# Twelve DRAM copies issued by ScalarE instead of GpSimd, with an order table of their own

## The chip, the cores and the metric

The kernel runs on one core of one Trainium2 chip. The metric is the device time of one execution in microseconds. The core has a matmul engine (TensorE, PE), VectorE (DVE), ScalarE (ACT), GpSimd (POOL) and SyncE (SP), each with an instruction queue of its own that is worked off in order, and 16 DMA engines that all queues' transfers share.

## The reference

One decoder layer on 512 tokens of width 1024 in float32: two token mixers in parallel, a gated merge, an output projection, layer norm, then a gated FFN of width 2816 with a short convolution, and layer norm again. Cut to what matters:

```python
def conv_ffn(x, w_up, conv_w, w_down):
    h = causal_dwconv(x @ w_up, conv_w)          # w_up 1024 x 5632, conv of width 3
    gate, val = jnp.split(h, 2, axis=-1)
    return (jax.nn.silu(gate) * val) @ w_down    # w_down 2816 x 1024

def reference(x, w_in, ...):
    h = x @ w_in                                 # 1024 -> 5408
    y_a = nsa_attention(...) @ w_nsa_out         # sparse attention, 8 heads
    y_b = gated_deltanet(...) @ w_gdn_out        # gated DeltaNet, 4 heads
    mix = (sigmoid(gate_a) * y_a + sigmoid(gate_b) * y_b) @ w_o
    x = layer_norm(ALPHA * x + mix, ln1_g, ln1_b)
    return layer_norm(ALPHA * x + conv_ffn(x, ffn_w_up, ffn_conv_w, ffn_w_down), ln2_g, ln2_b)
```

## The kernel before

Every large product is made in three passes: a float32 operand is cast to a high part (`wh`, `mh`, ScalarE or GpSimd) and the rest is a low part (`wl`, `ml`, VectorE), and PE adds high·high, high·low and low·high. A weight tile is loaded by SyncE into `raw` (3 buffers), cast into `wh` (3 buffers) and its rest into `wl` (3 buffers); then come 12 matmuls of it.

Three products are made with 7 half-size products in place of 8: the output projection with w_o, the down projection, and 7 of the 22 pairs of column groups of the up projection (`SEVEN`: pairs 5, 7, ... 17; function `seven`, one tile of 128x512 for each half-size product). The other pairs are made by `plain` with whole products. A half-size product of this kind needs sums of blocks of the weights. They are made by DMA in DRAM: each of `osum` (512 rows of 2 KB), `usum` (896 rows) and `wsum` (1408 rows) gets four sums by eight transfers. Four of the eight are plain copies (from the weight, or from one sum to the next), four add a block of the weight to what the copy left. Sums 0 and 1 are copied and added to; sum 2 is a copy of sum 1 with a block added, sum 3 a copy of sum 2 with a block added. All 24 are issued by GpSimd in before. SyncE loads the finished sums like other weights (`raw<-osum`, `raw<-usum`, `raw<-wsum`).

In time: until about 400 us the input projection and the two mixers run side by side, with `osum` and `usum` made beside them; then the merge (`mt`, L1147) and the w_o product with loads of `osum`; from about 450 the layer norm, which writes `mh` and `ml`, and with it the first up products; up to 700 the FFN's up projection, in which groups of `plain` and `seven` alternate and `wsum` is made; then the down projection, which reads `wsum`, and the last norm.

In `seven` the seven half-size products of a pair go through PSUM tiles `px`, `pz0` and `pz1`; after each, ScalarE or VectorE moves or adds it into the collecting tiles `wf0` and `wf1` (one buffer each), and the next product into the same PSUM tile waits for that. `gated` makes the convolution: `fa` by ScalarE (L1545), then two steps of VectorE (L1548). `fth` is the gate times the value: ScalarE (L1606), VectorE (L1607), GpSimd (L1608); `pha` is its high part (L1612, L1619), `pla` its low part.

The order of all instructions on each engine is fixed by a table `QUEUES`: for each engine a list of numbers, in which the n-th instruction that the program writes for this engine is number n. `queues` adds an ordering without a semaphore between neighbours of each list. So an instruction that waits holds back all that the table puts behind it on its engine.

Of the kernel before, what the change touches and what calls it, by code (L numbers as in the profile page):

```python
# [143 lines left out]
391-392 377 393 378 394 379-382 395 383 299-300 396-399 444-445 301 446-450 400-401 416 402-406 417 407-411 418-433
456 434-439 457-459 451 316-317 320 318 321-323 319 460-463 324-327 464-466 328 332-339 329-331 467-472 513 340-347
473-475 348-355 452 476-477 501 356-359 384-387 478-479 514-519 412-415 502-503 520-521 504 522-525 440 453 441 454
442 455 443 526-531 723-725 532 480-484 505 507-508 726-729 533 730 506 485 731 534-536 486-487 509-510 541 732 542
488-489 733-734 490 751-752 735-736 491-492 543 753 737 754-755 493 544 511 494 512 738 495 546-547 739 496 545 497
740 756-757 548 498-499 549 758-760 500 550-551 761 560-561 762 741 763-764 742-744 562 565 552 745 566 746 563-564
537 591 765 592 766 538-540 567 767 581-582 768 553-554 593 568 594-597 569 555 570 598-600 556-557 583 558 585 584  # L150
559 586 571 796 769-772 572-574 587 575 601 773 602 797-798 588 576 799 774 589-590 603-607 800-803 577-578 651 579
804-805 580 652 806 608-611 807-810 620 811 653-654 621 612 622-625 812-813 626 613 814-817 864 614 865 615 627 641
628-630 616-618 642 619 866-868 643-644 869-870 645-646 631 871-875 632 876-877 633 647-650 699-700 818 634-635
878-879 636 880-882 701-702 704-705 637 703 883 638 884 639 885-886 706 640 887 718-719 707-709 720-722 819 838-839
710 655-657 659-660 658 661-662 840-843 854-855 663-666 711-716 667-678 856 717 844 858 845 679-686 860 846-849 859
687-694 861 857 1053 850 695-698 747-748 862 749-750 863 1054 936-938 851 939-946 775 1055-1057 776-779 947-949 780
1058-1059 950 781 951-953 782 954-957 977 783 978 958 784-785 1060 959 1072 786-787 979 1073 852 980 853 981 788
982-984 789-790 985-986 791-792 987-992 793 1061 993-994 1001 794-795 1062 995-1000 1002-1012 1074 820 824-825 821-822
1075 823 1076 1101 1063 1013 826-829 1102 830-831 1103 832-833 1104-1108 1064 1029-1031 1014 1032 1065 1033-1034 1066
1035-1039 1067 1015 834 1040-1042 835 1043 1016 1044-1045 836 1046 837 1047-1049 1017 1050-1052 1068 1018-1019 888-891  # L160
1069 1077-1082 1070 1083-1100 1020-1023 1071 1024 1109-1112 892 896-897 893 898 894 899 895 1203 1205-1208 900-903
1204 1113 1209 1114-1115 904-905 908-915 906-907 1116 1219 1117 1210 1220 1118 1211 1119-1120 1212-1215 1221 916-923
1222-1223 1216 1121 1224 924-931 1122 1217 932-935 1225 1123 1233-1234 1124-1125 960 1126-1128 961 1129-1130 962-963
1131-1133 1218 1134-1136 964 1226 965 1235-1236 1227-1228 966 1141-1143 1238 1144-1145 967-968 1239 1146-1149 969 1237
970 1240 1150-1152 971-972 1153-1154 1252 1179 1241 973 1242 1253 1155 1180 974 1181-1182 975 1243 1254-1256 976
1156-1157 1183-1184 1158 1257 1159 1185 1160-1161 1186 1258 1244 1162 1187 1163-1164 1188-1190 1245 1191-1193 1246
1025-1026 1137-1139 1259 1140 1260-1261 1027 1262 1028 1273 1247 1194 1274 1195 1283 1196-1197 1248-1249 1198-1199
1284 1250 1200 1285 1251 1201 1263 1202 1165 1275 1169 1286-1287 1277 1307 1288 1278 1264 1170 1308-1310 1289-1290
1311 1166 1279 1167 1171 1280 1172-1173 1168 1174 1276 1403-1404 1312-1317 1175 1405 1176-1178 1265 1281 1406 1282
1407 1318 1266-1267 1319 1408 1320 1268 1291 1269 1409 1292 1270-1272 1321-1327 1229 1328-1329 1293-1294 1231 1410  # L170
1422-1423 1330 1295 1230 1296 1411 1424-1425 1412 1426 1413 1427 1297-1299 1232 1300-1303 1414 1428 1304 1379 1305
1415 1380 1416-1417 1306 1418 1429-1432 1443-1444 1381-1386 1419-1421 1387-1389 1433-1434 1445 1447-1448 1435 1390
1436 1391 1437 1331 1449 1332 1446 1453 1438-1439 1450-1452 1440 1454 1392 1477 1393-1394 1441 1395-1397 1455 1458
1478 1459 1479 1442 1480 1398 1460 1456-1457 1461-1462 1333 1463 1399 1481 1400-1401 1482-1483 1472-1473 1484-1485
1402 1474-1476 1334 1486-1491 1501-1502 1464-1465 1492 1466-1467 1582 1468 1503 1469-1470 1583 1517 1493 1518
1494-1495 1471 1504 1335 1505-1506 1336-1342 1519 1507 1521-1522 1496-1497 1508 1343-1346 1520 1509-1511 1584
1347-1358 1523 1512-1514 1498 1585 1544 1499 1545 1500 1359-1366 1524-1525 1546-1548 1367-1374 1515 1610 1549-1550
1375-1378 1526 1611 1586-1587 1527 1551-1552 1612 1588 1563 1528 1553 1529 1613 1554 1530 1589 1564 1590-1591 1614
# [189 lines left out]
def body(ctx: ExitStack, tc: tile.TileContext, d, out):  # L368
# [140 lines left out]
    def sums_o():  # L509
# [4 lines left out]
        for (to, src, add), u in zip(todo, SUMS):  # L514
            i = G.dma_start(out=osum[to], in_=src, **({"accum_op": OP.add} if add else {}))
# [1251 lines left out]
```

## Time and profile before

| | before |
|---|---|
| median of 3 runs | 837.82 us (837.53 to 840.38) |
| profiled execution | 837.5 us, its span 835.7 us, 12479 instructions |
| mean clock granted to PE | 0.992 |
| busy: PE, DVE, ACT, POOL | 97%, 77%, 52%, 23% |
| DMA | 139.8 MB moved; hardware queue q1 34.8% of 16 engines, GpSimd's queue q0 24.2% |

The span runs from the first to the last instruction of the profiled execution. Busy times are sums over an engine. q1 holds what SyncE issues; q0 what GpSimd issues. A line such as L1504 is a line of the kernel before; in the kernel after the same code stands one line further on. `a <- b` in a row of waits reads: the first waited for the second.

### The profile page before, as it was taken

What the parts mean: (1) busy time and instruction counts of PE and PEld (TensorE: products, weight loads), DVE (VectorE), ACT (ScalarE), POOL (GpSimd) and SP (SyncE); (2) the same over time, 40 slices, a digit from 0 to 9 for tenths busy, and PEclk for the clock granted to TensorE, in tenths of its full rate; (3) what the DMA queues carried; (4) which work ended last, traced back from release to release, by engine and by line L of the source; (5) the groups of instructions that cost most, each with busy time, mean ns of one, the idle gap of its engine ahead of it and who ended that gap; (6) DMA issues with size and microseconds to landing.
All of it is one profiled execution on the core that took longest, in us unless ns stands there. A gap on an engine that the chain in (4) does not pass through costs nothing.

```text
span 835.7 us, 12479 instructions
## 1 busy us (share of the span) xinstructions
PE 806.7 (97%) x4390; PEld 681.9 (82%) x4390; DVE 641.3 (77%) x1391; ACT 432.1 (52%) x965; POOL 195.2 (23%) x186
## 2 busy tenths in 40 slices
PE   9999999999999999999899999989999999999996
PEld 8788888778788888888787898968788888888875
DVE  5668689889678965565479879857777887788788
ACT  4463686774576764332344235543645654565541
POOL 0334825042275211332100112220011121100001
PEclk9999999999999999999999999999999999999999
DMA  8326129078246936446566697789483468475674
GB/s 277 95 86 214 30 76 249 26 192 186 56 131 156 187 90 153 151 127 153 213 252 203 239 185 234 182 220 201 137 276 114 140 156 197 138 206 173 205 238 148
DMA packets 53406, 139.80 MB, mean 167 GB/s; under 512 B 3936, under 2 KB 5088, under 8 KB 53088
## 3 DMA queue, kind: packets, MB, share of 16 engines
q1 hardware_dynamic: 36064, 92.88, 34.8%
q0 software_dynamic: 17280, 46.14, 24.2%
q8 instruction: 34, 0.56, 0.3%
q14 instruction: 28, 0.23, 0.1%
HBM read 136.91 MB, written 48.23 MB: 222 GB/s over the span
## 4 chain that ended last, share of the span: by engine, by line
PE 77%; DVE 10%; DMA 7%; ACT 3%; issue 2%; POOL 0%; SPq 0%; DVEq 0%; ACTq 0%; POOLq 0%
PE pu L1568 15%; PE gps L495 8%; PE gps L497 8%; PE gps L498 8%; PE px L1645 4%; PE px L1515 4%; PE pz L1645 4%; PE pz L1515 3%; DMA raw<-in_up 2%; PE pout L1115 2%; PE aps L1101 2%; DMA raw<-usum 2%; PE pu L1645 2%; PE pm L495 2%; PE pm L497 2%
## 5 line engine op out<-in xcount | busy, mean ns | idle before, releaser
L495 PE MATMUL gps<-xh,wh 128*128 128x512 f32 x320 | 125.2, 402 | 3.1 <-ACT mt L1147 2.3
L498 PE MATMUL gps<-xh,wl 128*128 128x512 f32 x320 | 125.7, 400 | 0.0
L497 PE MATMUL gps<-xl,wh 128*128 128x512 f32 x320 | 125.1, 399 | 0.0
L1568 PE MATMUL pu<-mh,wh 128*128 128x512 f32 x208 | 80.4, 398 | 2.2 <-ACT wh L1562 2.2
L1568 PE MATMUL pu<-mh,wl 128*128 128x512 f32 x208 | 79.7, 399 | 1.0 <-DVE wl L1563 1.0
L1568 PE MATMUL pu<-ml,wh 128*128 128x512 f32 x208 | 79.8, 396 | 0.0
L1608 POOL TENSOR_TENSOR fth<-fth,fa 128x512 f32<-128x512 f32 x22 | 32.4, 1474 | 197.3 <-DVE fth L1607 150.6
L495 PEld LDWEIGHTS gps<-xh,wh 128*128 128x128 f32 x320 | 60.5, 190 | 15.1 <-issue 3.3
L485 DVE TENSOR_TENSOR wl<-raw,wh 128x512 fp32r<-128x512 f32 x66 | 48.4, 738 | 29.7 <-PE gps L498 13.6
L498 PEld LDWEIGHTS gps<-xh,wl 128*128 128x128 f32 x320 | 60.5, 190 | 11.5 <-POOL wl L485 0.6
L497 PEld LDWEIGHTS gps<-xl,wh 128*128 128x128 f32 x320 | 60.5, 190 | 10.4
L1470 ACT ACTIVATE wh<-raw 128x512 fp32r<-128x512 f32 x67 | 39.9, 626 | 38.9 <-PE px L1645 9.5
L1562 ACT ACTIVATE wh<-raw 128x512 fp32r<-128x512 f32 x52 | 32.6, 628 | 51.5 <-PE pu L1568 41.5
L1471 DVE TENSOR_TENSOR wl<-raw,wh 128x512 fp32r<-128x512 f32 x67 | 44.4, 691 | 16.7 <-ACT wh L1470 16.6
L1563 DVE TENSOR_TENSOR wl<-raw,wh 128x512 fp32r<-128x512 f32 x52 | 38.2, 739 | 21.3 <-ACT wh L1562 18.1
L1504 ACT ACTIVATE wh<-raw 128x512 fp32r<-128x512 f32 x49 | 30.6, 628 | 40.2 <-PE px L1515 15.2
L1548 DVE SCALAR_TENSOR_TENSOR fa<-pu,fcw,fa 128x511 f32<-128x511 f32 (+1 forms) x60 | 44.3, 745 | 7.7 <-ACT fa L1545 7.4
L481 ACT ACTIVATE wh<-raw 128x512 fp32r<-128x512 f32 x46 | 28.8, 627 | 38.4 <-PE gps L497 29.6
L1568 PEld LDWEIGHTS pu<-mh,wh 128*128 128x128 f32 x208 | 39.7, 191 | 8.8 <-ACT wh L1562 2.6
L1568 PEld LDWEIGHTS pu<-mh,wl 128*128 128x128 f32 x208 | 39.6, 191 | 8.8 <-DVE wl L1563 2.6
L485 POOL TENSOR_TENSOR wl<-raw,wh 128x512 fp32r<-128x512 f32 x30 | 41.8, 1413 | 19.9 <-PE gps L498 5.4
L1568 PEld LDWEIGHTS pu<-ml,wh 128*128 128x128 f32 x208 | 39.6, 190 | 6.2
(498 smaller groups left out, 2252.8 us busy)
## 6 DMA issues: line engine op xcount, KB each, us to landing
raw<-in_wT SPq DMA_DIRECT2D x40, 512.0 KB, 3.7
raw<-in_up SPq DMA_DIRECT2D x37, 512.0 KB, 4.6
wsum<-in_down POOLq DMA_DIRECT2D x6, 2816.0 KB, 21.7
usum<-in_up POOLq DMA_DIRECT2D x6, 1792.0 KB, 15.8
raw<-wsum SPq DMA_DIRECT2D x20, 512.0 KB, 3.6
raw<-in_down SPq DMA_DIRECT2D x15, 512.0 KB, 4.3
osum<-in_wo POOLq DMA_DIRECT2D x6, 1024.0 KB, 10.8
wsum<-wsum POOLq DMA_DIRECT2D x2, 2816.0 KB, 15.0
```

What stands on the lines that cost most here:

```text
L485: eng.tensor_tensor(wl, r, wh.bitcast(F32), op=OP.subtract)
L495: i = PE.matmul(ps, wh[k], mh_(k), start=(k == 0), stop=False)
L497: PE.matmul(ps, wh[k], ml_(k), start=False, stop=False)
L498: PE.matmul(ps, wl[k], mh_(k), start=False, stop=(k == n - 1))
L1470: A.activation(hi, raw[:, i], AF.Copy)
L1471: V.tensor_tensor(lo, raw[:, i], hi.bitcast(F32), op=OP.subtract)
L1515: stop=k == 3 and w is lo) if False else PE.matmul(
L1548: V.scalar_tensor_tensor(acc[:, n:], ps[:, :S - n], w[:, i:i + 1], acc[:, n:], op0=OP.mult, op1=OP.add)
L1562: A.activation(hi, r, AF.Copy)
L1563: V.tensor_tensor(lo, r, hi.bitcast(F32), op=OP.subtract)
L1568: q = PE.matmul(ps, w[:, j], x[:, k, :], start=k == 0 and i == 0, stop=k == KD - 1 and i == 2, skip_group_check=True)
L1645: m = PE.matmul(ps, a[x](j)[:, ts], w[y], start=first and i == 0, stop=last and i == 2, skip_group_check=True)
```

## The change

The copies in the three functions that make sums are issued by ScalarE, the additions stay on GpSimd:

```diff
 def sums_o():
     ...
     for (to, src, add), u in zip(todo, SUMS):
-        i = G.dma_start(out=osum[to], in_=src, **({"accum_op": OP.add} if add else {}))
+        i = (G if add else A).dma_start(out=osum[to], in_=src, **({"accum_op": OP.add} if add else {}))
 def sums_u():
     ...
     for (to, src, add), u in zip(todo, SUMS_U):
-        i = G.dma_start(out=at(to), in_=src, **({"accum_op": OP.add} if add else {}))
+        i = (G if add else A).dma_start(out=at(to), in_=src, **({"accum_op": OP.add} if add else {}))
 def sums(n, after):
     ...
     for to, src, add in todo:
-        i = G.dma_start(out=wsum[to], in_=src, **({"accum_op": OP.add} if add else {}))
+        i = (G if add else A).dma_start(out=wsum[to], in_=src, **({"accum_op": OP.add} if add else {}))
```

GpSimd's list loses 12 entries and ScalarE's gains 12. The half-size products for 7 up pairs are in both kernels. The lists of all five engines are new; of each, one line:

```diff
 QUEUES = {
-    "Activation": """0-6 8 7 9-10 31 12-13 11 14 16 15 20 23 26 21-22 17 33 18 27 24-25 28 19 34-35 30 41 36 42 29 43-45 37-40 46 51 61 52
+    "Activation": """0-6 8 7 9-10 31 12 11 14 13 16 15 20 26 17 27 21 23 33 24 18-19 22 28 25 34-35 29-30 41 36 42-45 37-40 46 61 51-52 62
...
-    "Pool": """2 1 0 8 10 9 12 3 11 13 4 15 5-7 16-17 19 113 20-22 27-28 14 33 25 23 34 29 39 30-32 18 43 40 44 24 41 115 26 54 45 35
+    "Pool": """2 1 0 8-9 3 10-13 4 15 5-7 16-17 14 19-22 27-28 33 25 23 18 29 34 30 39 36 31-32 38 43 40 24 44 105 54 35 41 45 55 26
```

GpSimd in before, in the FFN's up projection (some 540 to 620 us); numbers behind a name tell its instances apart, and the instance numbers are the same in both kernels:

```order
L539 DMA wsum2_102<-in_down 1408x1x512
L1608 TENSOR_TENSOR fth_5675<-fth_5675,fa1_5671 128x512
L1608 TENSOR_TENSOR fth_5911<-fth_5911,fa1_5907 128x512
L539 DMA wsum0_100<-in_down 1408x1x512
L1608 TENSOR_TENSOR fth_5860<-fth_5860,fa1_5856 128x512
L1608 TENSOR_TENSOR fth_6096<-fth_6096,fa1_6092 128x512
L1608 TENSOR_TENSOR fth_6147<-fth_6147,fa1_6143 128x512
L1608 TENSOR_TENSOR fth_6332<-fth_6332,fa1_6328 128x512
L1608 TENSOR_TENSOR fth_6383<-fth_6383,fa1_6379 128x512
L539 DMA wsum3_103<-wsum2_102 1408x512
```

Three transfers of `wsum` stand among the FFN's products here; only the first is still among them in the new list.

GpSimd in after, from the end of the merge (400 us) to 520 us:

```order
L540 DMA wsum0_100<-in_down 1408x1x512
L552 TENSOR_TENSOR rs_5036<-rs_5036,minus_half_333 128x1
L552 TENSOR_TENSOR rs_5047<-rs_5047,minus_half_333 128x1
L552 TENSOR_TENSOR rs_5173<-rs_5173,minus_half_333 128x1
L552 TENSOR_TENSOR rs_5162<-rs_5162,minus_half_333 128x1
L540 DMA wsum1_101<-in_down 1408x1x512
L1609 TENSOR_TENSOR fth_5470<-fth_5470,fa1_5466 128x512
L1441 TENSOR_TENSOR sr0a_5441<-mh_4006,ml_4007 128x1024
L1448 TENSOR_TENSOR sr1a_5442<-sr0a_5441,sr1a_5442 128x1024
L1609 TENSOR_TENSOR fth_5485<-fth_5485,fa1_5481 128x512
```

The addition into `wsum0` stood between the products `fth_5911` and `fth_5860` and now stands ahead of the layer norm's `rs`; the copies into `wsum1` and `wsum3` are no longer in the list.

ScalarE in before, at 560 us:

```order
L1606 ACTIVATE fth_5911<-fa0_5903 128x512
L1619 ACTIVATE pha_5439<-fth_5911 128x2x256
L1545 ACTIVATE fa1_6092<-pu1_5984,fcw_324 128x512
L1539 ACTIVATE wf0_5942<-px1_5939 128x256
L1562 ACTIVATE wh_6159<-raw_6157 128x512
L1504 ACTIVATE wh_6182<-raw7_6180 128x512
L1612 ACTIVATE pha_5439<-fth_5860 128x256
L1562 ACTIVATE wh_6199<-raw_6157 128x512
L1504 ACTIVATE wh_6221<-raw7_6180 128x512
```

Of these rows `pha_5439<-fth_5911` moves back, and `wf0_5942` and `wh_6159` move up.

ScalarE in after, from the same `fth_5911` on:

```order
L1607 ACTIVATE fth_5911<-fa0_5903 128x512
L1540 ACTIVATE wf0_5942<-px1_5939 128x256
L1563 ACTIVATE wh_6159<-raw_6157 128x512
L1546 ACTIVATE fa1_6092<-pu1_5984,fcw_324 128x512
L1505 ACTIVATE wh_6182<-raw7_6180 128x512
L1563 ACTIVATE wh_6199<-raw_6157 128x512
L1613 ACTIVATE pha_5439<-fth_5860 128x256
L1546 ACTIVATE fa0_5980<-pu0_5920,fcw_324 128x512
L1505 ACTIVATE wh_6221<-raw7_6180 128x512
L1546 ACTIVATE fa0_6139<-wf0_5942,fcw_324 128x512
L1620 ACTIVATE pha_5439<-fth_5911 128x2x256
```

`pha_5439<-fth_5911`, which reads what GpSimd makes of `fth_5911`, stood right behind the `fth_5911` of ScalarE and now stands behind `wh_6221`; `wf0_5942` and `wh_6159` follow directly.

ScalarE in after, at the copy into `wsum1` (some 470 us; `mh` are the parts of the layer norm's output, transposed by PE):

```order
L1295 ACTIVATE mh_4006<-pt_5101 128x4x128
L1373 ACTIVATE wh11_5207<-raw_5205 128x1024
L540 DMA wsum1_101<-in_down 1408x1x512
L1295 ACTIVATE mh_4006<-pt_5151 128x4x128
L1295 ACTIVATE mh_4006<-pt_5260 128x4x128
```

The copy, on GpSimd's list before, is new between `wh11` and the next `mh`.

ScalarE in after, at the copy into `wsum3` (some 635 us):

```order
L1505 ACTIVATE wh_6830<-raw_6828 128x512
L1563 ACTIVATE wh_6867<-raw_6865 128x512
L1546 ACTIVATE fa0_6688<-pu0_6628,fcw_324 128x512
L540 DMA wsum3_103<-wsum2_102 1408x512
L1546 ACTIVATE fa1_6800<-pu1_6692,fcw_324 128x512
L1505 ACTIVATE wh_6890<-raw7_6888 128x512
L1563 ACTIVATE wh_6907<-raw_6865 128x512
```

Here too only the copy is new to ScalarE, among the casts for `seven` and `plain`; in before GpSimd issued the copy into `wsum1` at 458.6 us and that into `wsum3` at 610.5 us.

The other copies on ScalarE's new list, by the instructions beside them: `osum1` near 85 us, `usum` near 137, 142, 178 and 279, `osum2` near 177, `osum0` near 206, `osum3` near 315, `wsum0` ahead of the merge's `mt` at 401, `wsum2` near 513.

More of the change, by code (lines that the diff above doesn't have):

```diff
@@ L144 @@
[L144 to L178, printed above, removed]
@@ new lines @@
+2029 2011 2033 2042 2012-2016 2034-2035 2017 2036 2043 2037 2044 2038 2045 2039 2046 2040 2047 2041 2048-2049
+2054-2055 2050 2056-2058 2051 2059-2061 2052 2062 2053 2063 2066-2068 2064 2072 2069-2070 2073-2074 2065 2071
+2075-2077 2081-2082 2093 2090 2094 2091 2095 2117 2078 2114 2092 2115 2096 2083 2116 2097 2118 2099-2100 2119 2098
+2101 2120-2121 2102 2123 2079 2124 2122 2105 2126 2106 2125 2087 2127 2103 2080 2107 2129 2084 2088-2089 2111
+2085-2086 2104 2108 2112 2141 2130 2142 2128 2143 2109 2147 2132 2131 2110 2113 2133-2135 2148 2136 2149 2137-2140
@@ new lines @@
+2283 2316 2284 2346-2347 2317 2285 2318-2320 2286 2348-2350 2287 2257-2258 2321 2259 2351 2260-2261 2288-2289 2352
+2262 2290 2322 2353 2263 2291 2323 2292 2324 2264-2265 2354 2325 2293 2266 2294 2326 2355 2295 2356 2327 2357-2358
+2298-2305 2267-2270 2296 2328 2359 2297 2360 2329-2333 2271 2361 2272-2273 2334-2337 2386 2410 2362 2434-2435
+2411-2412 2436 2387 2413 2437-2438 2414 2363-2366 2388 2367 2415 2439 2368-2370 2389 2416 2440 2390 2371 2417
+2391-2392 2372 2393 2441-2443 2418 2394-2396 2444 2373 2419 2374-2377 2397-2398 2445-2446 2420 2399-2400 2378
@@ new lines @@
+4018 4016-4017 4021-4022 4019-4020 4024 4023 4025-4027 4030-4032 4036 4028-4029 4033-4035 4039-4040 4037 4041 4045
+4038 4042-4044 4046-4047 4051-4052 4048-4050 4053-4057 4060 4058-4059 4061-4073 4099-4100 4074-4075 4101-4102 4076
+4103 4077-4078 4104 4079-4081 4105-4109 4082 4110 4083-4097 4111 4098 4112-4131""",
+    "DVE": """0 27 104 1-4 6 5 7 9 8 10-11 13 12 14-17 58 18 59-60 19 61 23 21 64-65 22 66 20 26 62 31 90 32 67 63 33 72 34 30 35-36
+24 37 73 38-52 74 53-54 68-71 83 29 84 55 81 92 82 93 91 85-86 115 56 87 94 88 95 75 80 25 151 153 76 152 154 77 102
@@ L345 @@
+102-103 105-115 118 116 119 117 120-122 125 123-124 126-129 132 130-131 133-136 139 137-138 140-155 157-178 156
+179-186 188 190 192 194-201 187 193 202-203 189 191 204-205""",
 }
```

357 lines of the change are left out of this document (188 added, 169 removed).

## The prediction

> **What bounds the kernel now.** I read the head of the page first, then the chain that ended last, then the waits of the matmul engine, then stretches of 10 us around those waits, and last the transfers.
>
> ```profile
> span 835.7 us, 12479 instructions
> PE 806.7 (97%) x4390; PEld 681.9 (82%) x4390; DVE 641.3 (77%) x1391; ACT 432.1 (52%) x965; POOL 195.2 (23%) x186
> PE 77%; DVE 10%; DMA 7%; ACT 3%; issue 2%; POOL 0%; SPq 0%; DVEq 0%; ACTq 0%; POOLq 0%
> ```
>
> PE is busy for 806.7 of 835.7 us, so whatever the change does to other engines counts only where PE stands still or runs at a lower clock: at most 29.0 us. POOL has 0% of the chain and its queue 0%. What PE waits for between 400 and 700 us, where the FFN's half of the sums is made (columns: us in total, times, longest):
>
> ```profile
> PE gps L495 <- ACT mt L1147: 2.3, 1, 2.3
> PE pu L1568 <- ACT wh L1562: 2.2, 2, 1.2
> PE px L1515 <- ACT wf L1529: 2.0, 1, 2.0
> PE px L1515 <- ACT wf L1524: 1.8, 1, 1.8
> PE px L1515 <- ACT wh L1504: 1.2, 1, 1.2
> PE pu L1568 <- DVE wl L1563: 1.0, 2, 0.8
> PE px L1515 <- DVE wf L1534: 0.9, 1, 0.9
> PE pu L495 <- ACT mh L1294: 0.2, 1, 0.2
> ```
>
> These eight make 11.6 us, nearly all on ScalarE's casts. The stretches in which they lie (us, busy time and count of PE, PEld, DVE, ACT, POOL, the granted clock, DMA share, GB/s):
>
> ```profile
> 540.00:550.00 10.00, 8.21 (x42) 7.06 (x41) 8.38 (x15) 5.19 (x10) 0.00 (x0) 0.83 1.11 243
> 560.00:570.00 10.00, 8.05 (x38) 6.37 (x37) 5.12 (x9) 4.70 (x9) 3.14 (x3) 0.83 1.05 237
> 580.00:590.00 10.00, 8.03 (x54) 7.10 (x53) 6.39 (x12) 4.36 (x9) 2.63 (x2) 1.00 0.71 239
> 620.00:630.00 10.00, 7.96 (x51) 7.03 (x51) 4.25 (x8) 3.23 (x7) 1.29 (x1) 1.00 0.58 174
> 640.00:650.00 10.00, 10.00 (x69) 9.10 (x68) 8.95 (x15) 4.41 (x9) 0.00 (x0) 1.00 0.41 133
> ```
>
> PE loses 1.8 to 2.0 us in each of the first four and nothing in the last. In two the clock is 0.83 as well: 17% of 10 us, 1.7 us more each. The DMA share goes with it: over 1.0 where a sum's transfer runs.
>
> **The 12 issues leave POOL.** Durations are least/median/greatest in ns; the plain copies are the short ones of each group, the accumulating ones the long.
>
> ```profile
> L515 POOL DMA_DIRECT2D osum<-in_wo x6: 782/1214/1247, 128.9 to 381.4; - x6
> L515 POOL DMA_DIRECT2D osum<-osum x2: 707/714/722, 227.8 to 307.0; - x2
> L529 POOL DMA_DIRECT2D usum<-in_up x6: 971/1522/1552, 65.4 to 307.7; - x6
> L529 POOL DMA_DIRECT2D usum<-usum x2: 834/858/882, 179.2 to 246.7; - x2
> L539 POOL DMA_DIRECT2D wsum<-in_down x6: 1061/1723/1771, 400.5 to 680.9; - x6
> L539 POOL DMA_DIRECT2D wsum<-wsum x2: 914/916/917, 507.9 to 610.5; - x2
> ```
>
> Two of each row: 2 × (0.78 + 0.71 + 0.97 + 0.86 + 1.06 + 0.92) = 10.6 us off POOL, which is 23% busy and on no part of the chain: 0 us. The Trainium skill speaks to this in "DMA: Bandwidth & Descriptors", section "Issuing engines are not separate DMA queues": transfers started from ScalarE, SyncE and GpSimd run on the same 16 DMA engines, so another issuer saves only sequencer time. By it the change alone is worth nothing, which the 0% agree with; I keep it as a rival.
>
> **They arrive on ScalarE.** The trace shows no DMA issued by ScalarE. The nearest are SyncE's loads of the same rows of 2 KB, 128 and 256 of them at a time:
>
> ```profile
> L1497 SPq DMA_DIRECT2D raw<-usum x7: 326/326/327, 519.5 to 662.5; - x7
> L1198 SPq DMA_DIRECT2D raw<-osum x8: 359/377/679, 386.3 to 446.7; - x8
> ```
>
> By these, 128 more rows cost 33 ns. The copies have 512, 896 and 1408 rows: 0.42, 0.52, 0.65 us, together 4 × 1.59 = 6.4 us; with no slope 12 × 0.33 = 4.0. ACT is 52% busy. The one copy without cover is the second of wsum, between the casts `mh` L1294 at 470 us, where PE already waits 0.2 us for ACT: I take +0.4, between 0 and 0.65. The first of wsum stands ahead of `mt`, for which ACT idles 7 us:
>
> ```profile
> 401.41 0.60 ACT L1147 ACTIVATE mt<-gps 128x512 f32<-128x512 f32 x1 [7.04 <-DVE mt L1228]
> ```
>
> so it is free, and the 2.3 us of PE there stay, since what it waits for is unchanged.
>
> **ACT now waits for an addition.** The third copy of wsum reads what the second's addition wrote. Copied at 470.5, landed about 15 us later, added with some 22 us:
>
> ```profile
> wsum<-wsum POOLq DMA_DIRECT2D x2, 2816.0 KB, 15.0
> wsum<-in_down POOLq DMA_DIRECT2D x6, 2816.0 KB, 21.7
> ```
>
> gives 507 to 509; ACT comes there at 512.8. Behind it stand `fa` L1546 and the casts of 517 us, so it must be some 6 us late before PE notices: 0.
>
> **The traffic moves, and loads with it.** In before, wsum0's addition is issued at 560.1 and the fourth copy at 610.5. Two loads of one and the same size, in and out of these:
>
> ```profile
> 560.09 1.73 POOL L539 DMA_DIRECT2D wsum<-in_down  x1
> 610.49 0.92 POOL L539 DMA_DIRECT2D wsum<-wsum  x1
> 616.39 0.33 SPq L1497 DMA_DIRECT2D raw<-usum  x1
> raw<-usum SPq DMA_DIRECT2D x2, 256.0 KB, 8.6
> 641.26 0.33 SPq L1497 DMA_DIRECT2D raw<-usum  x1
> raw<-usum SPq DMA_DIRECT2D x2, 256.0 KB, 2.7
> 624.24 0.63 ACT L1504 ACTIVATE wh<-raw 128x512 fp32r<-128x512 f32 x1 [3.76 <-DMA raw<-usum]
> 624.78 0.37 ACT L1529 ACTIVATE wf<-px 128x256 f32<-128x256 f32 x1
> ```
>
> Beside the copy the pair lands in 8.6 us, alone in 2.7: 5.9 us late. ACT idles 3.76 us for it, and `wf` behind the cast is the one for which PE waits 2.0. After the change the addition follows its copy at once (415 to 440 us) and the fourth copy goes out near 635. From 556 to 633 no sum is on the way. So the waits that late loads made go: the 2.0 at 623, and the 1.2 at 578 (`px <- ACT wh L1504`), where the cast starts as a load of 571.1 lands beside the addition (the second line is the time from issue to landing):
>
> ```profile
> L1497 SPq DMA_DIRECT2D raw<-usum x1: 326/326/326, 571.1 to 571.1; - x1
> DMA to landing us min/median/max: 7.4/7.4/7.4
> ```
>
> Together −3.2. Of the 580s, where 1.97 are lost beside the addition's end, half: −1.0.
>
> The fourth copy now covers the loads of 641 and 646, on time today. A load 5.9 us late lost PE 2.0 at 623; I take +2.0 here, between 0 and 2 × 2.0. The addition now covers the loads of `osum` at 417 to 440:
>
> ```profile
> 420.00:430.00 10.00, 10.00 (x46) 8.27 (x45) 6.98 (x12) 2.87 (x6) 0.00 (x0) 1.00 0.81 291
> ```
>
> PE loses nothing there and the DMA engines are 0.81 full; a loss is possible, 0 to 2.0, and I take the middle, +1.0.
>
> **ScalarE's new order.** At 560 us `pha` stands ahead of three casts, and ACT idles for GpSimd's product:
>
> ```profile
> 560.18 0.63 ACT L1619 ACTIVATE pha<-fth 128x512 fp32r<-128x512 f32 x1 [3.02 <-POOL fth L1608]
> ```
>
> In the new order it stands nine places later, so the 1.95 us that the stretch 560 to 570 loses and its 1.7 of clock should go: −3.7. At 545 `wf` waits for `fa` on DVE; the `fa` that read it come earlier now, by DVE's list, but DVE is 84% busy there: half of 1.79 + 1.7, −1.8. All lists differ, in the attention part too. In PE's row of 40 slices only the last is far from full:
>
> ```profile
> PE   9999999999999999999899999989999999999996
> ```
>
> Of the 29.0 us without a matmul, the waits listed are 11.6 and the end, 0.3 to 0.4 of its 20.9 us, some 7; about 10 are the start and small gaps that a list makes or spares. I take a third more of them, +3.0, between −3 and +6.
>
> **The sum.** +0.4 − 3.2 − 1.0 + 2.0 + 1.0 − 3.7 − 1.8 + 3.0 = −3.3 us. The profiled execution took 837.5 (span 835.7 and 1.8 around it), 0.3 below the median of 837.82: 837.5 − 3.3 = 834.2.
>
> **Rivals.** *ScalarE is held by its big copies* (slower). No transfer of the trace from a hardware queue has more than 256 rows; these have 1408. If an issue lasts until its descriptors are drained, its upper bound is the copy's landing, 15.0 us. A cast is made up to two tiles ahead: 12 matmuls of 0.40 us (4.8) and 12 of half the columns (2.4), less the cast of 0.63, so some 6 us cover the copies at 513 and 635, 7 the one at 401, and nothing the one at 470. Fully held: 15 + 9 + 9 + 8 = +41. Held half as long, 7.5 us: 7.5 + 1.5 + 1.5 + 0.5 = +11, and with the gains above 845. It decides from about 3.5 us of issue on, which eats the gain at 470 alone. Against it: 33 ns per 128 rows. "Perfetto Trace Analysis" in the Trainium skill, section "DMA Instruction — HWDGE (DVE, Sync)", says that the descriptor generator is locked for one transfer and shared between issuers, and that its buffer can fill before generation ends; by that SyncE's loads would stand behind the copy too. No row here shows such a lock. Chance 0.14.
>
> *The collisions have only moved* (slower): each of the loads at 417 to 440, at 641 and at 646 costs PE 2.0 and one clock step of 1.7, 11.1 in all instead of +3.0, and the 545 gain stays out (+1.8): 834.2 + 8.1 + 1.8 = 844. For it: both places are full or on time today; against: the 2.1 us of 623 took no clock step. 0.07.
>
> *Nothing happens* (same): the gaps named are replaced by as many elsewhere, since only POOL's free time was saved: 837 to 838. For it, 0% POOL. 0.23.
>
> *All of it closes* (faster): 545 goes fully (−1.7 more), the loads at 641 and in 417 to 440 have slack (−3.0), so 834.2 − 4.7 = 829.5. 0.14.
>
> **How the numbers follow.** My forecast has 0.42. A measurement here tells 0.5%, 4.2 us, from no change: faster is below 833.6, slower above 842.0. The forecast's own range, 831 to 838, lies half below 833.6: 0.2 faster, 0.22 same. With the rivals: faster 0.2 + 0.14 = 0.34, same 0.22 + 0.23 = 0.45, slower 0.21. The range 829.5 to 843 leaves out the held ScalarE and the far edge of the moved collisions.
>
> **What would show it.** Right: no wait of PE for ACT at 561, 578 and 623, clock 1.00 from 550 to 640, ACT's 12 issues below 0.7 us each, POOL's busy time down by 10 us or so. Wrong: an ACT issue of several us, or idle time of ACT ahead of wsum's third copy (the first rival); loads of `usum` that land 8 us after issue near 641 with PE waiting for `wf` or `wh` behind them (collisions moved); a gap of 2 us still at 545 or 561 though ACT's order there is the new one; new gaps in the attention part of over 3 us in all.

## The result, and the profile after

The changed kernel took 842.76 us in the median of 20 runs (838.08 to 849.69), the kernel before 837.67 in 20 runs (835.60 to 840.38): slower, with a ratio of 1.0070 (95% interval 1.0046 to 1.0094). I had forecast 834.2. The profiled execution of after took 848.17 us, one of its longer ones. The head of its page, its chain by engine and its two queues for sums (packets, MB, share of 16 engines):

```profile
span 846.4 us, 12491 instructions
PE 816.5 (96%) x4390; PEld 685.0 (81%) x4390; DVE 636.2 (75%) x1391; ACT 435.7 (51%) x965; POOL 186.9 (22%) x174
PE 77%; DVE 11%; DMA 5%; ACT 3%; issue 2%; POOL 1%; SPq 0%; DVEq 0%; ACTq 0%; POOLq 0%
q0 software_dynamic: 11456, 23.07, 15.8%
q10 hardware_dynamic: 11456, 23.07, 8.3%
```

Half of the sums' bytes now go through ScalarE's queue q10, and POOL is busy 8.3 us less. PE is busy 9.8 us longer for the same matmuls, so the clock is to be looked at, and the place of the loss. This is worked out from the two traces: points at which PE had finished the same set of matmuls in both, in us from the start, and the difference as it is and without the time that half-clock windows (stretches in which PE was granted half its clock) cost up to there:

```
before   after   after-before   same, at full clock
 67.8     68.3      +0.5            +0.5
123.6    131.9      +8.4            +1.5
167.2    178.6     +11.4            +2.9
397.1    410.7     +13.5            +5.0
457.1    470.1     +13.0            +4.5
480.5    497.3     +16.8            +8.3
540.1    556.5     +16.4            +7.9
641.8    649.4      +7.6            +2.5
703.6    711.7      +8.1            +2.9
827.7    838.1     +10.4            +5.3
```

The up projection, 540 to 642 us, gains 8.8 us, where the prediction looked for gains. PE's waits there in after (us in total, times, longest):

```profile
PE pu L1569 <- ACT wh L1563: 1.3, 2, 1.0
PE px L1516 <- DVE wf L1535: 1.0, 1, 1.0
PE pz L1516 <- ACT wh L1505: 0.9, 1, 0.9
PE px L1516 <- ACT wh L1505: 0.6, 1, 0.6
PE pu L1569 <- DVE wl L1564: 0.3, 1, 0.3
```

They make 4.1 us where before's six, in the same stretch, made 9.1, and both half-clock windows are gone. The loss lies elsewhere: 13.5 us by the merge, 3.8 in the layer norm, 2.3 from 704 to 828. The largest piece, at 90 to 110 us (columns as in the prediction: after, then before):

```profile
90.00:100.00 10.00, 8.88 (x69) 6.67 (x68) 4.04 (x9) 4.84 (x14) 6.41 (x5) 0.75 0.19 62
100.00:110.00 10.00, 10.00 (x46) 7.68 (x46) 2.62 (x9) 3.39 (x12) 5.48 (x6) 0.57 0.09 22
```

```profile
90.00:100.00 10.00, 10.00 (x93) 7.62 (x92) 6.02 (x14) 6.28 (x22) 7.34 (x6) 1.00 0.18 54
100.00:110.00 10.00, 10.00 (x57) 8.45 (x56) 9.22 (x35) 9.35 (x39) 5.62 (x5) 1.00 0.33 91
```

A clock of 0.75 and 0.57 is 2.5 + 4.3 = 6.8 us. PE's rows there in after:

```profile
93.18 1.07 PE L820 MATMUL dps<-ym,x 128*128 128x64 f32 x8 [0.61 <-DVE ym L817]
94.77 0.72 PE L686 MATMUL dps<-ident,z 128*128 128x128 f32 x3 [0.52 <-DVE z L821]
96.08 0.53 PE L832 MATMUL dps<-z,m 32*32 32x32 f32 x12
96.54 0.80 PE L499 MATMUL gps<-xh,wl 128*128 128x512 f32 x1
```

From 91.2 to 96.5 only small DeltaNet matmuls run, in a row with two waits; in before, 512-wide matmuls of the input projection stand between them.

Every run lists its span and mean granted clock. Span times clock is its **full-clock span**, the rest is **lost to the clock**. After: 833.5 us at full clock in the mean, lost 8.2, in two groups (9 runs 2.5 to 5.9, 11 runs 9.2 to 13.5). Before, in the five sets of runs of the experiments: 829.3 to 830.0 at full clock, lost 6.8 to 7.3. So of the difference of the means nearly 4 us are there at full clock, and about 1 is clock, which makes most of the spread.

### The profile page after: what moved, and what is told of

It is laid out like the page before. It is cut to its first block, busy times and chain, and to the rows that moved or that the text cites. A ratio compares the mean times of both kernels' runs of the same rounds, so it can differ in the third digit from the quotient of the medians.

```text
span 846.4 us, 12491 instructions
## 1 busy us (share of the span) xinstructions
PE 816.5 (96%) x4390; PEld 685.0 (81%) x4390; DVE 636.2 (75%) x1391; ACT 435.7 (51%) x965; POOL 186.9 (22%) x174
## 3 DMA queue, kind: packets, MB, share of 16 engines
q0 software_dynamic: 11456, 23.07, 15.8%
## 4 chain that ended last, share of the span: by engine, by line
PE 77%; DVE 11%; DMA 5%; ACT 3%; issue 2%; POOL 1%; SPq 0%; DVEq 0%; ACTq 0%; POOLq 0%
PE pu L1569 15%; PE gps L496 8%; PE gps L499 8%; PE gps L498 8%; PE px L1516 4%; PE px L1646 4%; PE pz L1516 3%; PE pout L1116 2%; PE pz L1646 2%; PE pu L1316 2%; PE pw L1316 2%; PE pm L496 2%; PE pm L499 2%; PE aps L1102 2%; PE pm L498 2%
## 5 line engine op out<-in xcount | busy, mean ns | idle before, releaser
L486 DVE TENSOR_TENSOR wl<-raw,wh 128x512 fp32r<-128x512 f32 x66 | 50.1, 763 | 19.3 <-ACT wh L482 9.9
L1472 DVE TENSOR_TENSOR wl<-raw,wh 128x512 fp32r<-128x512 f32 x67 | 46.4, 711 | 18.1 <-ACT wh L1471 17.7
L1564 DVE TENSOR_TENSOR wl<-raw,wh 128x512 fp32r<-128x512 f32 x52 | 37.7, 726 | 16.0 <-ACT wh L1563 13.3
L1506 DVE TENSOR_TENSOR wl<-raw,wh 128x512 fp32r<-128x512 f32 x49 | 35.6, 728 | 14.2 <-ACT wh L1505 12.7
L486 POOL TENSOR_TENSOR wl<-raw,wh 128x512 fp32r<-128x512 f32 x30 | 39.2, 1309 | 26.0 <-PE dps L891 10.0
## 6 DMA issues: line engine op xcount, KB each, us to landing
wsum<-in_down POOLq DMA_DIRECT2D x4, 2816.0 KB, 24.2
wsum<-in_down ACTq DMA_DIRECT2D x2, 2816.0 KB, 14.9
wsum<-wsum ACTq DMA_DIRECT2D x2, 2816.0 KB, 15.2
```

What stands on the lines that cost most here:

```text
L486: eng.tensor_tensor(wl, r, wh.bitcast(F32), op=OP.subtract)
L1472: V.tensor_tensor(lo, raw[:, i], hi.bitcast(F32), op=OP.subtract)
L1506: E("ul", 10 * p + i).tensor_tensor(lo, r, hi.bitcast(F32), op=OP.subtract)
L1564: V.tensor_tensor(lo, r, hi.bitcast(F32), op=OP.subtract)
```

## The experiments

Order and issuer can be had apart: the tables number instructions by engine, and a list can be put together from stretches of both kernels' lists, each in its own order. "Full" and "lost" are the means' differences to before in the same set (errors 0.35 to 0.9 and 0.5 to 1.0 us; 5 to 12 runs of each kernel).

| kernel | median us | ratio (95%) | full | lost |
|---|---|---|---|---|
| e1_issuer | 845.90 | 1.0094 (1.0061 to 1.0127) | +4.9 | +2.5 |
| e2_order | 842.14 | 1.0052 (1.0028 to 1.0075) | +4.6 | −0.6 |
| e3_old400 | 840.32 | 1.0017 (0.9992 to 1.0043) | +1.9 | −0.1 |
| e4_old125 | 851.37 | 1.0157 (1.0128 to 1.0186) | +9.1 | +3.3 |
| g1_norm | 839.70 | 1.0020 (1.0004 to 1.0036) | +4.0 | −2.4 |
| g2_up | 837.94 | 1.0000 (0.9985 to 1.0015) | +0.6 | −0.9 |
| g3_down | 840.16 | 1.0022 (1.0000 to 1.0044) | +1.5 | +0.6 |
| g4_upact | 837.66 | 0.9990 (0.9974 to 1.0006) | +0.5 | −1.1 |
| h1_up706 | 834.25 | 0.9951 (0.9929 to 0.9974) | −1.9 | −2.1 |
| h2_att | 846.63 | 1.0092 (1.0064 to 1.0121) | +6.5 | +1.4 |
| h3_port | 840.33 | 1.0033 (1.0012 to 1.0055) | +1.4 | +1.7 |
| h4_issuer2 | 841.88 | 1.0046 (1.0018 to 1.0074) | +2.2 | +1.9 |
| i1_up706 | 834.16 | 0.9952 (0.9928 to 0.9976) | −1.5 | −2.9 |
| i2_att1 | 845.27 | 1.0071 (1.0043 to 1.0099) | +2.5 | +3.5 |
| i3_att2 | 843.04 | 1.0051 (1.0027 to 1.0075) | +3.1 | +1.1 |
| i4_pe | 841.96 | 1.0028 (1.0003 to 1.0054) | +4.7 | −2.2 |
| j1_wo_up | 834.73 | 0.9961 (0.9938 to 0.9985) | −2.5 | −1.1 |
| j2_early | 835.25 | 0.9951 (0.9929 to 0.9974) | −2.1 | −1.6 |

**Issuer and order apart.** My first theory was that the loss is order in the first 400 us and the issuer is free; the rival, that ScalarE's issues cost it.

```diff
 e1_issuer
-            i = G.dma_start(out=osum[to], ...)
+            i = (G if add else A).dma_start(out=osum[to], ...)     # and usum, wsum; lists of before
```

> The order of before on all engines; only the 12 copies are issued by ScalarE, each put into ScalarE's list at the time at which GpSimd issued it in before. Theory (the loss is in the new order of the first 400 us, where PE drops to half its clock; who issues the copies is free): 837 to 839 us, within 0.3% of before, ACT's 12 issues 0.5 to 0.7 us each. Rival (ScalarE's issues or the second hardware queue cost the time): 841 us or more.

```diff
 e2_order
-            i = (G if add else A).dma_start(out=osum[to], ...)
+            i = G.dma_start(out=osum[to], ...)                     # and usum, wsum; lists of after
```

> The order of after on all engines, with the 12 copies put back into GpSimd's list at the time at which ScalarE issued them in after. Theory (order): slower than before by 0.4 to 1%, 841 to 846 us, with half-clock windows near 95 us in its profile in some runs and a spread of several us. Rival (issuer): 837 to 839 us, no such windows.

After's order alone gives 842.14, after with ScalarE's issues 842.76: there the issuer is free, and the order costs 4.6 us at full clock. But in before's order the issuer cost 4.9 us: e2 came at the number of the theory and e1 at that of the rival, so neither holds for both orders. Matched to before, e1 runs within 0.1 us of it up to 117 us and takes on its full-clock loss at two places only (another 0.8 after 560). The first, at 125 us, is one VectorE instruction, the scaling of `sc`. All of them in before (least/median/greatest ns), then the one at 125 and GpSimd's subtraction beside it in before, and both in e1:

```profile
L1085 DVE TENSOR_SCALAR sc<-sc,mn,gsig x26: 327/475/5099, 106.0 to 285.2; 128x512 f32<-128x512 f32 x9, 128x128 f32<-128x128 f32 x8, 128x384 f32<-128x384 f32 x5, 128x256 f32<-128x256 f32 x4
```

```profile
123.65 2.58 DVE L1085 TENSOR_SCALAR sc<-sc,mn,gsig 128x512 f32<-128x512 f32 x1
123.94 2.00 POOL L485 TENSOR_TENSOR wl<-raw,wh 128x512 fp32r<-128x512 f32 x1
```

```profile
123.73 5.15 DVE L1085 TENSOR_SCALAR sc<-sc,mn,gsig 128x512 f32<-128x512 f32 x1
124.14 2.01 POOL L485 TENSOR_TENSOR wl<-raw,wh 128x512 fp32r<-128x512 f32 x1
```

(The 5.1 us of the first row are another one, at 169.7 us, as long in e1.) In e1 the scaling begins 0.08 us later and the subtraction 0.20 us later, in a row of back-to-back GpSimd work; PE's gap behind it grew from 1.33 to 3.90. This comes again: ten profiles with before's lists at this place and GpSimd as the issuer have 2.55 to 2.58 us, the three with ScalarE as the issuer (e1, e3, h4) 5.14 to 5.15. That the shift in time makes the difference is inferred. The second place is the layer norm: ScalarE's copy of wsum 1 was issued at 458.1, ahead of a load of up weights by SyncE; in before GpSimd issued it at 458.6, behind the last of them (457.9). PE's row in e1, and that line's loads in before, e1 and h4 (issues, then time to landing):

```profile
471.61 0.39 PE L495 MATMUL pu<-mh,wh 128*128 128x256 f32 x1 [3.21 <-ACT mh L1294]
```

```profile
L1369 SPq DMA_DIRECT2D raw<-in_up x4: 327/336/346, 448.3 to 457.9; - x4
DMA to landing us min/median/max: 3.6/4.4/5.6
```

```profile
L1369 SPq DMA_DIRECT2D raw<-in_up x4: 328/336/345, 450.8 to 460.4; - x4
DMA to landing us min/median/max: 4.4/5.1/8.6
```

```profile
L1369 SPq DMA_DIRECT2D raw<-in_up x4: 327/336/346, 452.2 to 461.7; - x4
DMA to landing us min/median/max: 4.1/4.3/5.0
```

8.6 us in place of 5.6, and `mh` stands behind the cast that waits for it. The next kernel moves that copy alone, behind the `mh` casts:

```diff
 h4_issuer2: ScalarE's list, against e1_issuer
-L539 DMA wsum_101<-in_down 1408x1x512
 L1294 ACTIVATE mh<-pt 128x4x128
 L1372 ACTIVATE wh_5207<-raw 128x1024
 L1372 ACTIVATE wh_5200<-raw 128x1024
 L1294 ACTIVATE mh<-pt 128x4x128 x3
+L539 DMA wsum_101<-in_down 1408x1x512
```

> The order of before with all copies on ScalarE, as the issuer kernel, but the second copy of wsum stands behind the casts of the layer norm (after SyncE's loads of the up weights) and not ahead of them. Theory (of the 5 us that the issuer kernel lost at full clock, 2.9 are these loads, landed late beside the copy, and 2.4 the scaling on VectorE at 124 us): 2.5 to 3 us less at full clock than that kernel, no gap of 3 us at 468. Rival (a hardware-queue copy slows whatever is loaded beside it, wherever it stands): no gain, the gap moves to another place.

The 3 us gap is gone and full clock is 2.7 us better than in e1 (+2.2 against +4.9). What is left is the scaling at 124 us, 5.1 us here too. So this copy cost PE 3 us where a load that PE soon needed stood behind it, and not where it stood behind the loads. Which part of it is the place and which the queue was not tried apart, since e1 changed both.

**The scaling by itself.**

```diff
 h3_port: in split_w, for two weight tiles
+        if next(CALLS) in (14, 16):
+            eng = V
```

> Before, with four subtractions wl (two weight tiles, at 124 to 128 and 168 to 171 us) on VectorE in place of GpSimd. They stand in rows of back-to-back GpSimd work beside which one VectorE instruction, the scaling of sc at L1085, took 2.6 and 5.1 us against 0.47 in the median. Theory (that instruction waits for a pause of GpSimd): both fall below 1 us, the PE gaps of 1.3 and 1.7 us behind them shrink, 1 to 3 us less at full clock. Rival (the scaling is long for another reason, such as where its data lie): both stay long and the time is that of before or more, as VectorE has 2.7 us more to do.

The row in this kernel:

```profile
L1090 DVE TENSOR_SCALAR sc<-sc,mn,gsig x26: 332/472/760, 105.8 to 287.6; 128x512 f32<-128x512 f32 x9, 128x128 f32<-128x128 f32 x8, 128x384 f32<-128x384 f32 x5, 128x256 f32<-128x256 f32 x4
```

None is above 0.76 us: the long ones came from the rows of GpSimd work. The time did not follow: the gap of 1.33 behind the scaling at 125 went (one of 0.75 for `dt` stands at 127), but a wait of 3.0 us for `acc` on VectorE came at 170. That GpSimd's work makes the scaling long held; the time came out at the rival's number.

**Two stretches put back in after.**

```diff
 e3_old400: the lists of all engines
-after
+before, for what it had started by 399 us; then after
 e4_old125
-after
+after to 68 us; before from there to 124 us; then after
```

> Copies on ScalarE; all engines in the order of before for what before had started by 399 us, then in the order of after. Theory: the first 400 us as in before, and of the rest the gain of 540 to 660 us (8.5 us between the two profiles) less the losses at 457 to 480 (3.8) and 750 to 811 (3.5): 1 to 3 us faster than before, 834.5 to 837 us. Rival (the loss comes from the copies or is spread over the program): 840 us or more.

> The order of after, with one stretch of all engines (68 to 124 us) in the order of before. Theory (the half-clock stretch of 13.7 us at 95 us follows from a run of small products there): that stretch is gone in every profile, median 4 to 8 us below after, 835 to 839 us, and a spread of 2 us in place of 11. Rival (the clock falls for reasons outside this order, by chance or by the power drawn elsewhere): 841 to 844 us with the same spread, clock 0.984 to 0.997 again.

e3 came out at the rival's number; its profile has a scaling of 5.14 us and a PE gap of 3.90 there as in e1. e4 was a miss: the windows at 95 went, but my splice left ScalarE's first copy of osum behind the seam, and GpSimd's addition, which waits for it, held GpSimd's other work (GpSimd's wait, then PE's):

```profile
POOL osum L517 <- DMA osum<-in_wo: 11.5, 1, 11.5
```

```profile
PE aps L1103 <- DVE sc L1087: 9.3, 2, 8.4
```

It says nothing on the order of that stretch; it does show what an addition costs whose copy is late.

**Stage by stage**, with all copies on GpSimd unless said:

```diff
 g1_norm
-before
+before to 399 us; after through the layer norm; before from 480 us
 g2_up
-before
+before to 480 us; after to 690; before; wsum0's addition at 417 us
 g3_down
-before
+before to 700 us; then after
 g4_upact: as g2_up, and
+            i = (A if to in [2, 3] and not add else G).dma_start(out=wsum[to], ...)
```

> All copies on GpSimd. The order of before, but from the merge through the w_o product and the layer norm (399 to 480 us) that of after. New theory (before and after differ by stages: +5 us in the first 400, +4 in the layer norm, -5.5 in the up projection, +3.4 in the down projection, all at full clock; half-clock windows add a spread): +3 to +4 us at full clock over before. Rival (the loss of the layer norm in after comes from ScalarE's copy that stands there): 0 to +1 us.

> All copies on GpSimd. The order of before, but in the FFN's up projection (480 to 690 us) that of after, and wsum0's addition at 417 us, right behind its copy. New theory: 5 to 6 us less than before at full clock and fewer half-clock windows between 540 and 570, so 4 to 8 us faster than before (830 to 834 us). Rival (that gain needs the copies on ScalarE): within 2 us of before.

> All copies on GpSimd. The order of before to 700 us, then that of after (the down projection and the last norm). New theory: +2.5 to +3.5 us at full clock over before. Rival (after loses there only because it comes there with its sums later): 0 to +1 us.

> As the kernel with the order of after in the up projection alone, and the copies of wsum 2 and 3, which lie in it, issued by ScalarE at after's places. New theory (who issues is free where no load stands beside the copy): within 1 us of that kernel, 830 to 834 us. Rival (ScalarE's issue is what clears the loads): at least 2 us faster than it; third (ScalarE's copy crowds SyncE's loads): at least 2 us slower.

g1 lost its 4.0 us though GpSimd issues the copy, so after's loss in the stretch from the merge through the layer norm (399 to 480 us) is order (PE's waits in the layer norm):

```profile
PE pu L496 <- ACT mh L1295: 1.1, 2, 0.7
PE pt L1293 <- DVE x L1281: 1.0, 2, 0.6
PE pt L1293 <- DVE ml L1296: 0.8, 1, 0.8
```

g3 lost 1.5, between theory and rival. g2 gained nothing. Its waits of PE, GpSimd's issue and ScalarE's cast:

```profile
PE pu L1319 <- ACT woh L1205: 4.5, 1, 4.5
PE pw L1319 <- DVE x L1324: 1.5, 1, 1.5
```

```profile
416.71 1.72 POOL L543 DMA_DIRECT2D wsum<-in_down  x1 [12.87 <-DMA wsum<-in_down]
```

```profile
439.27 1.06 ACT L1205 ACTIVATE woh<-raw 128x1024 fp32r<-128x1024 f32 x1 [6.20 <-DMA raw<-osum]
```

The up projection has the clock of 1.00 and the smaller gaps of after, and the addition at 417 made the loads of `osum` late: the gain was paid back there. g4 equals g2 within 0.3 us: the issuer is free again.

**Where can the addition go?** Three more places, with g4's rest:

```diff
 h1_up706, against g4_upact
-wsum0's addition at 417 us
+wsum0's addition behind wsum1's, at 499.5 us
 i1_up706, against g4_upact
-wsum0's addition at 417 us
+wsum0's addition behind wsum3's, at 697.5 us
 j2_early, against g4_upact
-wsum0's copy at 400 us, its addition at 417 us
+its copy ahead of the addition at 336 us
 j1_wo_up, against g4_upact
+after's order from 399 to 448 us too, wsum0's addition at its place in it
```

> As the kernel with the order of after in the up projection and ScalarE's copies of wsum 2 and 3, but wsum0's addition goes out at 706 us, behind the last sum, and not at 417 beside the loads of osum. Theory (there, the addition delayed the loads of osum and cost the 4.6 us gap of PE at 434 and 1.5 at 456, which ate the gain of the new order): those gaps gone, full-clock span 824 to 826 us, time 830.5 to 834 us. Rival (the gain of 480 to 690 is not there, or its loss only moves to 706 to 730): 837 us or more.

The table of h1 was not what this text says: the addition went out at 499.5 us. GpSimd's rows and PE's wait:

```profile
477.69 1.77 POOL L543 DMA_DIRECT2D wsum<-in_down  x1
499.50 1.71 POOL L543 DMA_DIRECT2D wsum<-in_down  x1 [20.04 <-issue]
```

```profile
PE pu L1572 <- DVE fa L1552: 3.9, 1, 3.9
```

> Order of before, but in the up projection that of after, copies of wsum 2 and 3 by ScalarE; wsum0's addition really goes out behind wsum3's, near 706 us (the kernel before this one, meant to do that, issued it at 499.5, behind wsum1's, and GpSimd stood still for 20 us). Theory (the PE gap of 3.9 us at 501 was GpSimd standing): gap gone, 3 to 4 us less at full clock than that kernel, 823 to 825 us of full-clock span, time 829 to 833. Rival (the addition costs about the same wherever it runs beside loads): full-clock span 826.5 us or more, a new gap near 710 to 730.

The gap of 3.9 went, but PE waited behind the addition, at 712 to 718 us, and the full-clock span was no better than h1's:

```profile
PE px L1649 <- ACT wh L1474: 2.6, 2, 2.1
```

> Order of before, but that of after for the merge and the w_o product (399 to 448 us, with wsum0's addition at 419) and for the up projection (480 to 690); copies of wsum 2 and 3 by ScalarE. Theory (after's w_o order leaves the loads of osum ahead of the addition): full-clock span 824 to 826 us, clock lost 4 to 6, time 830 to 833 us, no gap over 1 us near 434. Rival (the gap at 434 comes back): 834 us or more.

> Order of before, but that of after for the up projection (480 to 690); copies of wsum 2 and 3 by ScalarE; wsum0's copy and addition issued by GpSimd at about 322 and 337 us. Theory (there is room beside the loads of the input projection): full-clock span 824 to 826 us, time 829 to 832 us. Rival (the addition delays the loads of the projection weights, or GpSimd's wait for the copy holds its work): full-clock 828 us or more, with a new gap between 325 and 365.

j1 lost 2.7 us at 453 (`pw <- DVE x`). j2:

```profile
PE pm L499 <- DVE mt L1230: 4.8, 1, 4.8
```

With the addition at each of these places PE has a wait of 2.1 to 4.8 us beside it or behind it. For j1 that the addition did it is not shown: it had landed at 437.2, and the gap stands at 453. None of the four came to the full-clock span that was expected of it (824 to 826 us, of i1 823 to 825): h1 827.4, i1 828.5, which is its rival's number, j1 827.0, j2 827.4. Their medians were 0.25 to 3.25 us above what was expected. By the medians all four still beat before and after: the up projection's order is worth more than what came with it.

**The attention part.**

```diff
 h2_att
-before
+after to 412 us; then before
 i2_att1
-before
+after to 177 us; then before
 i3_att2
-before
+before to 167 us; after to 412; then before
```

> All copies on GpSimd; the order of after until the merge (its first 412 us), then that of before. Theory (the first 400 us of after's order are slower at full clock, by 5 us in the profiles): +3 to +6 us of full-clock span over before, 841 to 845 us, with half-clock windows near 95 us in most runs. Rival (the first 400 us cost clock alone): full-clock span within 1 us of before.

> All copies on GpSimd; the order of after for its first 177 us, then that of before. Theory (from the profiles: 3.8 us of after's loss in the attention part are there, and the half-clock windows at 95): full-clock span +3 to +4.5 us over before, clock lost 1 to 3 us more, windows at 95 in the profile. Rival (the loss is made later): within 1.5 us of before at full clock.

> All copies on GpSimd; the order of before for 167 us, then that of after until the merge, then before again. Theory: full-clock span +1 to +2.5 us over before, no half-clock window before 160 us. Rival (the losses don't add by stages): 0 or less, or over +4.

6.5 us at full clock in h2, 2.5 and 3.1 in its halves, so both halves lose. h2 and i3 lost more than expected (3 to 6 and 1 to 2.5 us), i2 less (3 to 4.5), but 3.5 to the clock where 1 to 3 was expected. No single wait carries it: in h2's trace the loss against before grows by 0.2 to 1.6 us at a time, at 68 to 94, 124 to 167, 215 to 262 and 368 to 397 us, and 167 to 215 gives 1.5 back. Which rows of the lists make each of these stays open. i2's profile has no half-clock window at 95, against the expectation, though PE's lists there are the same and its two waits are 0.61 and 0.51 us:

```profile
90.00:100.00 10.00, 8.88 (x85) 6.83 (x84) 5.63 (x15) 5.99 (x17) 6.41 (x5) 1.00 0.24 82
```

Its 12 runs lost 7.5 to 15.2 us to the clock all the same.

```diff
 i4_pe: PE's list, against after (a part)
-L499 MATMUL gps_1199<-xh_93,wl_1193 128x512
-L496 MATMUL gps_1199<-xh_93,wh_1191 128x512
-L498 MATMUL gps_1199<-xl_94,wh_1191 128x512
...
 L815 MATMUL dps_905<-z_896,m_827 128x64 x2
+L499 MATMUL gps_1199<-xh_93,wl_1193 128x512
+L496 MATMUL gps_1199<-xh_93,wh_1191 128x512
+L498 MATMUL gps_1199<-xl_94,wh_1191 128x512
```

> After, with PE's order alone changed at one place: twelve of the 512-wide input-projection matmuls that ran ahead of the small DeltaNet matmuls of 91 to 96 us stand between them, four by four. Theory (5 us of small matmuls with 1.1 us of waiting make the clock fall there): the windows of 10 to 14 us at 95 are gone or shorter than 4 us, clock lost 2 to 5 us less than after's mean of 8.2, the median 838 to 841 us and less spread. Rival (the clock falls for the work that follows, or by chance): windows near 95 again, lost 7 to 9 us, 842 to 844 us.

```profile
90.00:100.00 10.00, 10.00 (x90) 7.69 (x89) 5.95 (x15) 5.82 (x17) 6.38 (x5) 1.00 0.18 64
```

The two gaps and the windows are gone; a wait of 1.10 us for GpSimd's `z`, ending at 89.7, stands and has no window. The 12 runs lost 1.7 to 7.6 us, mean 5.0, where after lost 2.5 to 13.5, mean 8.2, with 11 of its 20 at 9.2 or more. So the runs of after that lost most go with PE's order at this one place. It is not the only place that trips the clock: i3, with before's order up to 167 us, lost 5.9 to 12.7. The ratio to before of the same set fell from 1.0070 in after to 1.0028 here. The median of 841.96 lies a little above the 838 to 841 expected, since the span at full clock came out no shorter (+4.7).

## Why the prediction was wrong

The step that failed is the last of "ScalarE's new order": "All lists differ, in the attention part too ... I take a third more of them, +3.0, between −3 and +6." By stages the new lists cost 6.5 us in the attention part (h2), 4.0 from the merge through the layer norm (g1) and 1.5 in the down projection (g3): 12 us at full clock, and about 1 us more of lost clock in the mean. With the 5.4 us that the up projection gains at full clock that makes 6.6, where after stands 3.5 to 4.2 above before and e2 4.6; so the stages, each measured among before's lists, do not add up exactly.

I had priced a whole new order from before's idle time; that time says what a list can spare, not what another list can add. The 10 us that I called start and small gaps were not that either: 7.6 of them are waits of PE that before's trace lists in the first 400 us, 3.0 of these on the scaling. In after they are 10.4, only 2.8 more, just under my sign of wrong (new gaps of over 3 us), while that part lost 5.0 at full clock in the profile. The rest stands in no listed wait, and which rows make it stays open. The trace of before could not give the number, and the range of this one term was too narrow.

The other steps, one by one:

- **POOL's issues, 0 us:** right in after's order: e2 and after differ by 0.6 us in the median, and g4 and g2, with after's up projection, by 0.3. In before's order, e1, the change of issuer cost 4.9 us at full clock.
- **ScalarE's issues, 4.0 to 6.4 us of its time, +0.4 exposed:** the time is right, 6.5 us; what was exposed no run measures by itself. None of the twelve is above 0.69 us (least/median/greatest ns):

```profile
L516 ACTq DMA_DIRECT2D osum<-in_wo x2: 577/632/687, 85.4 to 215.7; - x2
L516 ACTq DMA_DIRECT2D osum<-osum x2: 477/494/512, 185.2 to 325.6; - x2
L530 ACTq DMA_DIRECT2D usum<-in_up x2: 551/559/567, 144.1 to 150.1; - x2
L530 ACTq DMA_DIRECT2D usum<-usum x2: 477/490/502, 186.8 to 290.6; - x2
L540 ACTq DMA_DIRECT2D wsum<-in_down x2: 577/582/587, 405.0 to 481.2; - x2
L540 ACTq DMA_DIRECT2D wsum<-wsum x2: 507/508/509, 528.5 to 640.4; - x2
```

  The size hardly matters: 512 rows cost as much as 1408, against my slope of 33 ns for 128. So the rival "ScalarE is held by its big copies" fell. The lock of the descriptor generator of which the Trainium skill speaks ("Perfetto Trace Analysis", "DMA Instruction — HWDGE (DVE, Sync)") cost no issue more than 0.69 us here; what did cost, in e1, was a load landing 3 us later.
- **ACT's wait for the addition of wsum 1, 0:** right; that copy went out at 528.5 without a wait.
- **The up projection, −3.2 − 1.0 − 3.7 − 1.8, and +2.0 at 641:** −7.7 forecast for 540 to 642 us, −8.8 found, 3.4 of it clock. The pieces fit less well than the sum, which is in part luck. Both clock steps at 545 and 561 are gone: all eleven profiles with after's lists in the up projection have a clock of 1.00 from 520 to 690, eight of the nine with before's 0.96 to 0.99. The waits of 1.20 at 578 and 2.04 at 623 are gone, as forecast, and all of the 1.97 of the 580s, of which I took half. But at 545 1.79 only shrank to 0.93, and at 561, for whose 1.95 I took everything, two waits of 0.98 and 0.99 stand in after (the two longest of its list above). After's PE there, and at the collision of 641:

```profile
560.00:570.00 10.00, 8.45 (x53) 7.09 (x52) 6.30 (x12) 4.90 (x10) 0.00 (x0) 1.00 1.11 249
570.00:580.00 10.00, 8.03 (x46) 6.54 (x47) 5.90 (x12) 3.94 (x9) 2.90 (x2) 1.00 0.62 202
640.00:650.00 10.00, 10.00 (x62) 8.89 (x61) 9.01 (x17) 7.67 (x14) 1.29 (x1) 1.00 1.04 365
```

  The collision cost PE nothing. That the gain is order and traffic, not the issuer, is what g2 and g4 show.
- **wsum0's addition beside the loads of osum, +1.0:** 0 in after, where PE is 10.00 of 10 busy from 420 to 430 and from 430 to 440; 6.0 in g2, in before's order. In after, too, three loads of `osum` go out behind the addition, at 423.6, 433.2 and 434.2, and take 9.9 to 12.1 us; but the first cast that reads one of them waits for PE and not for the load. These loads had slack. In g2 the cast waits for the load (its row at 439.27 stands above). The addition and that cast in after:

```profile
419.00 1.96 POOL L540 DMA_DIRECT2D wsum<-in_down  x1 [4.93 <-DMA wsum<-in_down]
442.04 1.06 ACT L1202 ACTIVATE woh<-raw 128x1024 fp32r<-128x1024 f32 x1 [0.99 <-PE pw L1316]
```

  The bound of 2.0 held for after's order and was too small for before's.
- **Collisions only moved:** this rival had the sign, but not the place: the loads at 417, 641 and 646 cost after nothing.

The chance that I gave to slower, 0.21, was for two mechanisms that both stayed out. That 842.76 lies inside my range of 829.5 to 843 is luck: its upper end came from the moved collisions, which cost nothing.

## What to carry to other kernels

Split a change that comes with a new order into its issuer and its order before you price it, and the order into stages: here the part that the change was named for was worth nothing in its own order (and cost 4.9 us in the old one), one stage of the order gained nearly 9 us in the profile and three others lost more. Compare spans at full clock and time lost to the clock apart, since a place that trips the clock in some executions only can hide or fake a gain of 1%. The large addition came with a new wait of PE in each kernel that moved it among before's lists (g2, h1, i1, j1 and j2), and with none at 419 us among after's, where the loads beside it had slack: look for such a stretch, and check the slack in the order that you will run.
